# Gram products of a two-layer decoder trunk, taken alternately from the upper and the lower 64 rows of the array

## The chip, the cores and the metric

The kernel runs on one core of one Trainium2 chip, as one launch. The metric is the device time of a launch in microseconds (us), as the median of several runs.

## The reference

Two layers over 512 tokens of width 1024. Each layer projects the normalised input once and gives its columns to three groups of heads that work in parallel: RWKV-7 time mixing (4 heads of 64), retention (4 heads of 64) and latent attention (8 heads). Their outputs are joined, projected and added to the input; a SwiGLU block follows. Cut to the two parts that the change touches:

```python
def rwkv7_step(state, inp):                     # scanned over 512 tokens
    rt, kt, vt, wt, kkt, at = inp
    sa = einsum('bhvk,bhk->bhv', state, -kkt)
    state = state * wt[:, :, None, :] + sa[..., None] * (kkt * at)[:, :, None, :] \
            + vt[..., None] * kt[:, :, None, :]
    return state, einsum('bhvk,bhk->bhv', state, rt)

# retention, chunks of 128 tokens
inner = einsum('bhnqd,bhnkd->bhnqk', qc, kc) * dmask[:, None]
inner = einsum('bhnqk,bhnkd->bhnqd', inner, vc)
cross = einsum('bhnqd,nbhde->bhnqe', qc * q_dec[:, None, :, None], R_prev)
y = inner + cross
```

All is float32.

## The kernel before

Activations lie transposed, features on the partitions and the 512 tokens in the free dimension. The weights stream from HBM block by block (`wnext`): SP issues the load of `wr`, ACT rounds it to `wh` (L375), and DVE forms the rest `wl = wr - wh` (L376). A weight block is used in units of three matmuls, `wh` with both halves of the activation and `wl` with its high half, each 128 rows by 512 tokens (`gemm`, tiles `pd` in PSUM). These big products fill most of the tensor engine's (PE's) time. The block with the retention values is narrower, 288 columns, and its units count 288 instead of 512.

The small work of the three head groups is written as Python generators (`rwkv`, `chain`, `group_norm`, `retnet`, `head`, `attend`). A generator yields a number from the table `T`, how much modelled PE time should pass before it goes on; `Driver` then lets others go, the big gemm last. The order of PE's stream is thus fixed when the kernel is built, from a modelled clock that every `mm` moves on; `keep_in_program_order` holds PE to it. The other engines take their instructions in an order that a scheduler settles at build time. On all engines an instruction that waits holds up those queued behind it.

PSUM has two pools of four one-bank tiles each: `pd` for the big gemm and `pm` for the rest (`psd()`, `psm()`, 128 x 512 float32). A fifth `psm()` waits until the first of the four tiles has been read for the last time.

The recurrence of RWKV-7 is done in chunks of 64 tokens. For each of the 4 heads and 8 chunks a Gram product of 128 x 128 with a contraction of 64 is made (L629): `BK[b]` and `AR[b]` hold two heads each, one on partitions 0 to 63 (`par` 0), one on 64 to 127 (`par` 1). A product therefore uses the upper or the lower 64 rows of the array, and the profile lists two matmul records for it. The loops run over `par`, then `b`, then `i`: four chunks make a block of four products in one `pm` tile. DVE takes the tile out with two masked multiplications of 128 x 256 (L632 into `GL`, L633 into `GR`), and `yield T["rwkv13"]` (0.5) lets one unit of the big gemm go between two blocks. Eight blocks make a layer. After the four of one `par`, SP stores `GL[par]` to the scratch tensor `ms_d` (L635). Behind the last block come the bonus products (`pm<-r,EX`, L640) and the transposes to token-major stacks. SP then loads the 32 x 32 diagonal blocks from `ms_d` into `dg` (L669), and DVE inverts them in 31 steps of two instructions (L679, L680), with a yield after each. Between these steps DVE does the angle tables (L435 to L450), the rotation of the latent attention's key (`kro`, L1010 to L1015; its transposes on PE are the first to need it) and the decayed keys of retention (`kt`, L794).

Retention (`retnet`) scores four chunks of 128 tokens per head (L815): for each pair of heads `b` and each `par` four products of 128 x 128, contraction 64, into one `pm` tile, then a multiplication by the decay mask on DVE (L817), then `yield T["retnet3"]` (0.7). `py` (L824 to L829) uses both heads' masked scores; its products with the values write 64 of the 128 columns, `par` 0 the left and `par` 1 the right half.

Of the kernel before, what the change touches and what calls it, by code (L numbers as in the profile page):

```python
# [16 lines left out]
ALU = mybir.AluOpType  # L17
AX = mybir.AxisListType

P = 128  # L20
# [16 lines left out]
# how much of the tensor engine's work a task leaves between its steps  # L37
T = {'tables1': 19.74, 'norm1': 0, 'p_rwkv': 4, 'p_ret': 1, 'p_head': 4, 'p_tab': 6, 'p_gn': 1, 'p_att': 5, 'p_kr': 6, 'angles1': 0, 'angles2': 3.0, 'angles3': 0.93, 'angles4': 0.65, 'angles5': 2.78, 'angles6': 11.0, 'rwkv1': 2.97, 'rwkv2': 5.34, 'rwkv3': 0, 'rwkv4': 0, 'rwkv5': 4.5, 'rwkv6': 2.0, 'rwkv7': 0, 'rwkv8': 4.0, 'rwkv9': 2.51, 'rwkv10': 1.31, 'rwkv11': 1.12, 'rwkv12': 4.2, 'rwkv13': 0.5, 'rwkv14': 0, 'rwkv15': 0.35, 'rwkv16': 0, 'rwkv17': 0.75, 'rwkv18': 15.07, 'rwkv19': 0, 'rwkv20': 1.0, 'rwkv21': 1.29, 'chain1': 0.9, 'chain2': 0.9, 'chain3': 1.17, 'group_norm1': 3.0, 'group_norm2': 2.5, 'group_norm3': 7.53, 'retnet1': 0.8, 'retnet2': 0, 'retnet3': 0.7, 'retnet4': 3.0, 'retnet5': 2.5, 'retnet6': 0, 'head1': 4.54, 'head2': 0, 'head3': 8.46, 'head4': 0.22, 'attend1': 0, 'key_rope1': 4.96, 'latent_norm1': 1.34, 'latent_norm2': 2.88, 'latent_norm3': 0}
# the engine of each elementwise step that several can do: d DVE, p Pool, a Activation
# [5 lines left out]
def shape_constants():  # L45
    """Constants that depend on shapes and hyper-parameters alone."""
# [10 lines left out]
    j = i % 64  # L57
# [28 lines left out]
# rows of the parameter matrix (one row = 128 consecutive values of a parameter)  # L86
# [15 lines left out]
class Driver:  # L102
    """Orders the PE stream: the first task whose wait (in PE time, or a condition) is over goes on."""
# [25 lines left out]
def lay_out(inp):  # L129
    """The inputs as the kernel reads them: reshapes, transposes and repeated columns only."""  # L130
# [47 lines left out]
def tile_trunk(ctx: ExitStack, tc: tile.TileContext, a: dict, out: bass.AP, dbg=None):  # L178
# [50 lines left out]
    def mm(o, lhsT, rhs, start=True, stop=True, cost=None):  # L229
        """A matmul that keeps its place in the PE stream."""  # L230
# [51 lines left out]
    def split(src, dst):  # L282
        """An exact hi/lo pair of float32r halves."""
# [4 lines left out]
    def halves(src, key, hi_from=None):  # L288
        """The exact hi/lo pair of a tile."""
# [17 lines left out]
    def norm_feed(t, g, acc, tag="acc"):  # L307
        """Square of tile t into acc and the g-scaled tile as an exact hi/lo pair."""
# [14 lines left out]
    def rsqrt(x, y=None):  # L323
        """1 / sqrt(x) of a whole tile, with one Newton step."""
# [7 lines left out]
    def inv_rms(accs, n, tag):  # L332
        """rsqrt(mean + eps) per token, the same in all partitions, from tiles of squares."""
# [7 lines left out]
    def norm(acc, st):  # L341
        yield T["norm1"]
# [9 lines left out]
    # the weights, in order of use, as exact hi/lo pairs two blocks ahead of their products  # L352
# [31 lines left out]
    def gemm(ps, w, x, ks, first=True, last=True, wsl=None):  # L384
        """ps += w^T x in three exact passes; ks = [(index in w, index in x)]."""
# [13 lines left out]
    def first_two(x):  # L399
        """Two products whose last contraction tile comes late."""  # L400
# [847 lines left out]
```

## Time and profile before

| what | value |
|---|---|
| median of 3 runs | 1428.18 us (1426.4 to 1428.36) |
| span of the profiled execution | 1423.1 us |
| mean granted clock of PE | 0.970 of full |
| PE busy | 1366.6 us (96%) |
| DVE busy | 799.1 us (56%) |
| ACT busy | 566.5 us (40%) |
| POOL busy | 267.2 us (19%) |
| masks L632 and L633 | 16 each, 0.41 us each |
| retention masks L817 | 8, 0.68 us each |

The span counts from the first to the last instruction of one execution; the median counts a whole launch, and lies 5.1 us above it. A row of the timeline of an engine gives start, duration, engine, line, operation, output and inputs by the program's names, the form (rows by columns of the array for a matmul, then its operand), and how many instructions of one kind followed each other (x); in brackets stands the idle time before it with the instruction that ended it. A line of a matmul is that of the helper `mm` (L231) or `tr` (L238), so products are told apart by names and forms: `64*128` are the Gram products. Durations of matmuls overlap, since the engine pipelines them; the distance from start to start is what one costs. A row of the view of stretches gives begin and end, length, busy time of PE, of its weight loads (PEld), DVE, ACT and POOL with instruction counts, then the granted clock, the share of DMA and GB/s.

### The profile page before, as it was taken

The numbers are of one execution on the slowest core, as the hardware profiler recorded it, in microseconds if no ns is written. First come the engines' busy times: TensorE is split into PE (matmuls) and PEld (weight loads), VectorE is DVE, ScalarE is ACT, GpSimd is POOL, SyncE is SP. The second block draws the span as 40 slices with busy tenths as digits, with TensorE's granted clock in tenths as the row PEclk, the third lists the DMA queues.
The fourth block names the chain that finished last, engine by engine and source line by source line (L and its number), as shares of the span: only waits on it lengthen the run. The fifth ranks groups of instructions, "written<-read, shape, count | busy, mean of one in ns | idle before, by whom it ended". The sixth has DMA issues, their size and how long they took to land.

```text
span 1423.1 us, 17218 instructions
## 1 busy us (share of the span) xinstructions
PE 1366.6 (96%) x6622; PEld 1074.5 (76%) x6622; DVE 799.1 (56%) x1167; ACT 566.5 (40%) x943; POOL 267.2 (19%) x233
## 2 busy tenths in 40 slices
PE   7989899899999999999999989999999999999996
PEld 5768666568788888888887776765788888888884
DVE  6665855775644345444556767657475434543443
ACT  7633353663432223222457134448263322322233
POOL 2142024222211011001213502332031200100111
PEclk9869999999999999999999899999999999999998
DMA  6324231202332232322342332312123333333321
GB/s 224 90 81 112 76 92 53 91 36 77 104 102 95 98 98 95 103 89 93 118 138 77 107 87 56 100 43 75 59 89 104 89 104 93 100 98 95 100 77 60
DMA packets 61738, 130.85 MB, mean 92 GB/s; under 512 B 24948, under 2 KB 27668, under 8 KB 61656
## 3 DMA queue, kind: packets, MB, share of 16 engines
q1 hardware_dynamic: 60280, 128.14, 29.1%
q8 instruction: 52, 0.85, 0.3%
q10 hardware_dynamic: 1232, 1.09, 0.2%
q0 software_dynamic: 144, 0.52, 0.1%
q14 instruction: 30, 0.25, 0.1%
HBM read 117.40 MB, written 9.18 MB: 89 GB/s over the span
## 4 chain that ended last, share of the span: by engine, by line
PE 83%; DVE 8%; ACT 4%; issue 3%; POOL 1%; DMA 0%; SPq 0%; DVEq 0%; ACTq 0%; POOLq 0%
PE pd L231 70%; PE pm L231 12%; PE pm L238 1%; DVE r L680 1%; ACT wh L375 1%; DVE u L320 1%; DVE r L679 1%; DMA wr<-in_wts_dram 0%; DVE wl L376 0%; ACT u L860 0%; DVE nmx L858 0%; DVE u L286 0%; DVE r L295 0%; DVE r L328 0%; DVE r L329 0%
## 5 line engine op out<-in xcount | busy, mean ns | idle before, releaser
L231 PE MATMUL pd<-u,wh 128*128 128x512 f32 x3048 | 963.6, 397 | 9.9 <-ACT wh L375 6.3
L231 PEld LDWEIGHTS pd<-u,wh 128*128 128x128 f32 x3048 | 571.2, 190 | 139.8 <-issue 8.3
L231 PE MATMUL pd<-u,wl 128*128 128x512 f32 x1524 | 598.8, 393 | 0.0
L375 ACT CAST wh<-wr 128x1024 fp32r<-128x1024 f32 (+3 forms) x206 | 208.6, 1015 | 547.0 <-PE pd L231 349.2
L231 PEld LDWEIGHTS pd<-u,wl 128*128 128x128 f32 x1524 | 289.3, 190 | 61.3 <-DVE wl L376 0.2
L376 DVE TENSOR_TENSOR wl<-wr,wh 128x1024 fp32r<-128x1024 f32 (+3 forms) x198 | 277.6, 1404 | 82.9 <-ACT wh L375 82.1
L1184 POOL TENSOR_TENSOR r<-r,r 128x512 f32<-128x512 f32 x44 | 62.3, 1416 | 584.3 <-ACT wh L375 337.5
L1183 DVE TENSOR_TENSOR r<-pd,rB 128x512 f32<-128x512 f32 x44 | 30.4, 691 | 133.7 <-PE pd L231 133.7
L1190 DVE TENSOR_TENSOR u<-u,pd 128x512 f32<-128x512 f32 x48 | 33.0, 687 | 125.8 <-PE pd L231 125.8
L231 PE MATMUL pm<-u,u 32*32 32x32 f32 (+7 forms) x856 | 97.3, 279 | 5.8 <-DVE u L607 4.3
L231 PEld LDWEIGHTS pm<-u,u 32*32 32x32 f32 (+4 forms) x856 | 70.1, 155 | 41.5 <-issue 25.2
L315 POOL TENSOR_TENSOR acc<-acc,r 128x512 f32<-128x512 f32 x37 | 56.8, 1534 | 221.5 <-ACT r L314 221.0
L1181 DVE TENSOR_TENSOR r<-pd,rB 128x512 f32<-128x512 f32 x44 | 30.4, 691 | 68.4 <-PE pd L231 68.3
L285 ACT CAST u<-r 128x512 fp32r<-128x512 f32 x52 | 32.2, 622 | 63.0 <-POOL r L1184 62.8
L231 PE MATMUL pd<-u,u 96*128 96x512 f32 (+3 forms) x128 | 47.7, 471 | 1.9 <-ACT u L860 1.3
L286 DVE TENSOR_TENSOR u<-r,u 128x512 fp32r<-128x512 f32 x52 | 36.4, 701 | 16.5 <-ACT u L285 16.3
L376 POOL TENSOR_TENSOR wl<-wr,wh 128x1024 fp32r<-128x1024 f32 (+1 forms) x8 | 19.7, 2460 | 116.8 <-ACT wh L375 98.9
L238 PE MATMUL pm<-ident,u 128*128 128x128 f32 x188 | 35.2, 295 | 2.7 <-ACT u L875 1.8
L858 DVE TENSOR_REDUCE nmx<-pd 128x1 f32<-128x512 f32 (+1 forms) x64 | 30.0, 481 | 12.1 <-PE pd L231 11.9
L320 DVE SCALAR_TENSOR_TENSOR u<-u,PC,u 128x512 fp32r<-128x512 f32 x24 | 34.5, 1450 | 3.0 <-ACT u L319 3.0
L238 PEld LDWEIGHTS pm<-ident,u 128*128 128x128 f32 x188 | 25.1, 153 | 9.5 <-ACT u L875 2.2
L745 POOL TENSOR_SCALAR sd<-Sb,dsc 64x64 f32<-64x64 f32 x48 | 23.9, 498 | 42.2 <-DVE Sb L746 33.6
(241 smaller groups left out, 1170.6 us busy)
## 6 DMA issues: line engine op xcount, KB each, us to landing
wr<-in_wts_dram SPq DMA_DIRECT2D x174, 512.0 KB, 3.5
wr<-in_wts_dram SPq DMA_DIRECT2D x22, 384.0 KB, 3.1
u<-in_xT_dram SPq DMA_DIRECT2D x7, 512.0 KB, 7.1
tb<-tab_d SPq DMA_DIRECT2D x8, 256.0 KB, 3.4
r<-r SPq DMA_DIRECT2D x32, 64.0 KB, 2.0
h_d<-u SPq DMA_DIRECT2D x4, 512.0 KB, 2.6
u<-h_d SPq DMA_DIRECT2D x4, 512.0 KB, 4.9
wr<-in_wts_dram SPq DMA_DIRECT2D x4, 432.0 KB, 3.1
```

The lines of the kernel that those rows point to most:

```text
L231: tc.keep_in_program_order(nc.tensor.matmul(o, lhsT, rhs, start=start, stop=stop, skip_group_check=True))
L238: tc.keep_in_program_order(nc.tensor.transpose(o, x, idn))
L285: act.copy(hi, src)
L286: E("e273").tensor_tensor(lo, src, hi.bitcast(F32), ALU.subtract)
L315: E("e302").tensor_tensor(acc, acc, q, ALU.add)
L320: dve.scalar_tensor_tensor(lo, t, g, hi.bitcast(F32), ALU.mult, ALU.subtract)
L375: act.copy(hi[:, z], t[:, z])
L376: (pool if on in POOL_LO else dve).tensor_tensor(lo[:, z], t[:, z], hi[:, z].bitcast(F32), ALU.subtract)
L1181: dve.tensor_tensor(t, gu[0], rB, ALU.mult)
L1183: dve.tensor_tensor(u, gu[1], rB, ALU.mult)
L1184: E("e1171").tensor_tensor(t, t, u, ALU.mult)
L1190: dve.tensor_tensor(hk(m), hk(m), ps, ALU.add)
```

## The change

In the recurrence the loop over `par` moves inside. A step takes two `pm` tiles, one per `par`, and makes eight products, one into the first tile from rows 0 to 63, one into the second from rows 64 to 127, in turns. Four masks follow on DVE, then one yield; four steps make a layer, with a unit of the big gemm behind each. Both stores to `ms_d` come behind the last step. Retention's scores do the same per pair of heads: two tiles, eight products in turns, then two masks with a yield behind each. Nothing of the values changes. `T` becomes a list with one table per layer, both as the one before; line numbers move by one to three.

```diff
-        for par in range(2):
-            rows = slice(par * 64, par * 64 + 64)
-            for b in range(2):
-                for i in range(2):
-                    ps = psm()
-                    for j in range(4):
-                        n = 4 * i + j
-                        mm(ps[:, j * P : (j + 1) * P], BK[b][rows, n, :], AR[b][rows, n, :])
-                    h0 = b * 8 + 4 * i
-                    v3 = ps.rearrange("p (j w t) -> p j w t", j=4, w=2)
-                    dve.tensor_tensor(GL[par][:, h0 : h0 + 4, :], v3[:, :, 0, :], gmv[:, 0:1, :].broadcast_to([P, 4, 64]), ALU.mult)
-                    dve.tensor_tensor(GR[par][:, h0 : h0 + 4, :], v3[:, :, 1, :], gmv[:, 1:2, :].broadcast_to([P, 4, 64]), ALU.mult)
-                    yield T["rwkv13"]
-            sp.dma_start(ms_d[:, par * 16 : par * 16 + 16, :], GL[par][0:64])
+        GH = (slice(0, 64), slice(64, 128))
+        for b in range(2):
+            for i in range(2):
+                pg = [psm(), psm()]
+                for j in range(4):
+                    n = 4 * i + j
+                    for ps, rows in zip(pg, GH):
+                        mm(ps[:, j * P : (j + 1) * P], BK[b][rows, n, :], AR[b][rows, n, :])
+                h0 = b * 8 + 4 * i
+                v3 = [ps.rearrange("p (j w t) -> p j w t", j=4, w=2) for ps in pg]
+                for par in range(2):
+                    dve.tensor_tensor(GL[par][:, h0 : h0 + 4, :], v3[par][:, :, 0, :], gmv[:, 0:1, :].broadcast_to([P, 4, 64]), ALU.mult)
+                    dve.tensor_tensor(GR[par][:, h0 : h0 + 4, :], v3[par][:, :, 1, :], gmv[:, 1:2, :].broadcast_to([P, 4, 64]), ALU.mult)
+                yield T[l]["rwkv13"]
+        for par in range(2):
+            sp.dma_start(ms_d[:, par * 16 : par * 16 + 16, :], GL[par][0:64])
...
         for b in range(2):
-            Sm = []
+            Sm, pg = [], [psm(), psm()]
+            for n in range(4):
+                tk = slice(n * P, (n + 1) * P)
+                for par in range(2):
+                    rows = slice(par * 64, par * 64 + 64)
+                    mm(pg[par][:, tk], ks[rows, b, tk], qs[rows, b, tk])
             for par in range(2):
-                hh = 2 * b + par
-                rows = slice(par * 64, par * 64 + 64)
-                ps = psm()
-                for n in range(4):
-                    tk = slice(n * P, (n + 1) * P)
-                    mm(ps[:, tk], ks[rows, b, tk], qs[rows, b, tk])
+                hh, ps = 2 * b + par, pg[par]
                 t = r2()
```

PE's order around the first blocks of layer 0, before. `pm` tiles with a number are Gram blocks (`u_632` is `AR[0]`, `u_633` is `BK[0]`), `pd` rows are the gemm's units:

```order
L231 MATMUL pd_702<-u_143,wl_506 128x512
L231 MATMUL pm_735<-u_632,u_633 128x128 x4
L231 MATMUL pd_702<-u_146,wh_505 128x512 x2
L231 MATMUL pd_702<-u_146,wl_506 128x512
L231 MATMUL pm_746<-u_632,u_633 128x128 x4
L231 MATMUL pd_764<-u_112,wh_600 128x512 x2
L231 MATMUL pd_764<-u_112,wl_601 128x512
L231 MATMUL pm_774<-u_673,u_674 128x128 x4
```

And now, from the first step's last products to the next step's:

```order
L232 MATMUL pm_735<-u_632,u_633 128x128
L232 MATMUL pm_736<-u_632,u_633 128x128
L232 MATMUL pd_702<-u_146,wh_505 128x512 x2
L232 MATMUL pd_702<-u_146,wl_506 128x512
L232 MATMUL pm_753<-u_632,u_633 128x128
L232 MATMUL pm_754<-u_632,u_633 128x128
```

Where four products into one tile stood between two units, eight now stand, each other one into the second tile; the step behind the next unit takes the third and the fourth tile of the pool.

DVE's order in layer 0, before, from the weight split ahead of the Gram masks to the second block's masks (`u_731` and `u_732` are `GL`, `u_733` and `u_734` are `GR`):

```order
L376 TENSOR_TENSOR wl_705<-wr_703,wh_704 128x1024
L295 TENSOR_TENSOR r_142_684<-r_139_680,r_141_683 128x512
L614 SCALAR_TENSOR_TENSOR r_140_681<-u_498,PC,u_294 128x512
L376 TENSOR_TENSOR wl_767<-wr_765,wh_766 128x864
L295 TENSOR_TENSOR r_144_689<-r_140_681,r_143_688 128x512
L978 TENSOR_TENSOR r_145_692<-pd_598,rB_259 128x512
L632 TENSOR_TENSOR u_731<-pm_735,C 128x256
L633 TENSOR_TENSOR u_733<-pm_735,C 128x256
L632 TENSOR_TENSOR u_731<-pm_746,C 128x256
L633 TENSOR_TENSOR u_733<-pm_746,C 128x256
```

And now:

```order
L377 TENSOR_TENSOR wl_705<-wr_703,wh_704 128x1024
L377 TENSOR_TENSOR wl_781<-wr_779,wh_780 128x864
L296 TENSOR_TENSOR r_142_684<-r_139_680,r_141_683 128x512
L615 SCALAR_TENSOR_TENSOR r_140_681<-u_498,PC,u_294 128x512
L296 TENSOR_TENSOR r_144_689<-r_140_681,r_143_688 128x512
L981 TENSOR_TENSOR r_145_692<-pd_598,rB_259 128x512
L634 TENSOR_TENSOR u_731<-pm_735,C 128x256
L635 TENSOR_TENSOR u_733<-pm_735,C 128x256
L634 TENSOR_TENSOR u_732<-pm_736,C 128x256
L635 TENSOR_TENSOR u_734<-pm_736,C 128x256
L634 TENSOR_TENSOR u_731<-pm_753,C 128x256
```

The second weight split has moved up by two rows; both tiles of a step are masked one after the other, and the masks of the second step follow at once.

SP's order behind the Gram products of layer 0, before (`r` rows are swaps for the rotation of retention's queries and keys, `u_919` is `dg`, `wr` is a weight):

```order
L635 DMA ms_d<-u_731 64x1024
L980 DMA r_158_754<-r_157_753 32x512 x4
L635 DMA ms_d<-u_732 64x1024
L980 DMA r_177_866<-r_176_865 32x512 x4
L372 DMA wr_1074<-in_wts_dram 128x1024
L669 DMA u_919<-ms_d 32x32x32 x4
```

And now (`u_890` is `dg`):

```order
L983 DMA r_160_768<-r_159_767 32x512 x4
L638 DMA ms_d<-u_731 64x1024
L638 DMA ms_d<-u_732 64x1024
L672 DMA u_890<-ms_d 32x32x32 x4
L373 DMA wr_1078<-in_wts_dram 128x1024
```

Both stores stand together, and the loads of the diagonal blocks follow at once, ahead of the weight that they stood behind.

More of the change, by code (lines that the diff above doesn't have):

```diff
@@ L339, in inv_rms, with norm @@
         return rsqrt(x, sm((P, S), tag=tag, bufs=1))
-    def norm(acc, st):
-        yield T["norm1"]
+    def norm(l, acc, st):
+        yield T[l]["norm1"]
         st["rB"] = inv_rms(acc if isinstance(acc, list) else [acc], D, "rB")
@@ L417, in tables @@
     def tables():
-        yield T["tables1"]
+        yield T[0]["tables1"]
         posi = r2((P, S), I32)
@@ L464, in tables @@
         ready["ret"] = True
-        yield T["angles5"]
+        yield T[0]["angles5"]
         yield from angles(None, True)
         ready["kr"] = True
-        yield T["angles6"]
+        yield T[0]["angles6"]
         co, si = yield from angles(c("invm"))
@@ L532, in rwkv @@
         k_ = rkv["k"]
-        yield T["rwkv5"]
+        yield T[l]["rwkv5"]
         kk = ur([P, 2, S])
@@ L749, in chain @@
             E("c736").copy(AR[b][:, n, 64:128], pY)
-            yield T["chain3"]
-        drv.spawn(T["p_gn"], group_norm(l, st, b))
+            yield T[l]["chain3"]
+        drv.spawn(T[l]["p_gn"], group_norm(l, st, b))
     def group_norm(l, st, b):
@@ L818, in retnet @@
                 Sm.append(t)
-                yield T["retnet3"]
-            yield T["retnet4"]
+                yield T[l]["retnet3"]
+            yield T[l]["retnet4"]
             py = psm()
@@ L863, in head @@
             (pool if ib == 2 else dve).tensor_scalar(pp[ib], pp[ib], rs, None, ALU.mult)
-            yield T["head2"]
-        yield T["head3"]
+            yield T[l]["head2"]
+        yield T[l]["head3"]
         ta, tb = ur([P, 1024]), r2()
@@ L879, in head @@
         if hh ^ 1 in st["PT"]:
-            drv.spawn(T["p_att"], attend(l, st, b))
+            drv.spawn(T[l]["p_att"], attend(l, st, b))
     def attend(l, st, b):
-        yield T["attend1"]
+        yield T[l]["attend1"]
         po = psm()
@@ L931, in dense @@
             mix = st["mix"]
-            drv.spawn(T["p_rwkv"], rwkv(l, st))
-            drv.spawn(T["p_ret"], retnet(l, st))
+            drv.spawn(T[l]["p_rwkv"], rwkv(l, st))
+            drv.spawn(T[l]["p_ret"], retnet(l, st))
             for hh in range(8):
-                drv.spawn(T["p_head"], head(l, st, hh // 2, hh % 2))
+                drv.spawn(T[l]["p_head"], head(l, st, hh // 2, hh % 2))
             pss = yield from first_two(xg)
-            drv.spawn(0, norm(acc, st))
+            drv.spawn(0, norm(l, acc, st))
             ps = psd()
```

83 lines of the change are left out of this document (42 added, 41 removed).

## The prediction

> **What bounds the kernel now.** First the page: the busy shares, and the chain of work that ended last.
>
> ```profile
> PE 1366.6 (96%) x6622; PEld 1074.5 (76%) x6622; DVE 799.1 (56%) x1167; ACT 566.5 (40%) x943; POOL 267.2 (19%) x233
> PE 83%; DVE 8%; ACT 4%; issue 3%; POOL 1%; DMA 0%; SPq 0%; DVEq 0%; ACTq 0%; POOLq 0%
> ```
>
> PE works 96% of the span and carries 83% of the chain: time taken off PE comes off the end, unless a wait takes its place. Next one group by line and form, and two of PE's waits:
>
> ```profile
> L231 PE MATMUL pm<-u,u 64*128 64x128 f32 x192 | 36.9, 349 | 5.8 <-DVE u L607 4.3 <-DVE u L633 1.5
> PE pm L238 <- DVE kro L1015: 6.6, 1, 6.6
> PE pm L231 <- DVE kt L794: 5.5, 5, 3.0
> ```
>
> The first row is the change's object: 192 matmul records for 96 Gram products (two each), on 64 of the 128 rows. The third figure of that row is idle time before the group: PE waited 4.3 us for the products' inputs (L607) and 1.5 us for a PSUM buffer (which L633 had to empty). The timeline of PE gives the stretch in layer 0:
>
> ```profile
> 82.10 1.34 PE L231 MATMUL pm<-u,u 64*128 64x128 f32 x8 [4.30 <-DVE u L607]
> 83.37 1.22 PE L231 MATMUL pd<-u,wh 128*128 128x512 f32 x2
> 84.95 2.07 PE L231 MATMUL pm<-u,u 64*128 64x128 f32 x8
> 86.95 1.22 PE L231 MATMUL pd<-u,wh 128*128 128x512 f32 x2
> ...
> 109.87 1.91 PE L231 MATMUL pm<-r,EX 128*128 128x512 f32 x4
> ```
>
> Eight blocks of four products (x8 records), and behind each a unit of the big gemm (three matmuls). From start to start a block takes 86.95 - 84.95 = 2.00 us and a unit 84.95 - 83.37 = 1.58; the bonus products (pm<-r,EX) begin at 109.87. Why this is slow, the view of stretches says; the first figure behind POOL's is the granted clock:
>
> ```profile
> 82.87:113.59 30.72, 30.72 (x95) 22.64 (x94) 15.54 (x30) 2.75 (x5) 5.92 (x6) 0.50 0.24 62
> 113.59:144.00 30.41, 26.85 (x168) 24.18 (x166) 18.02 (x26) 12.16 (x21) 10.66 (x10) 1.00 0.50 122
> 803.08:816.73 13.65, 13.65 (x52) 11.93 (x52) 7.01 (x14) 0.47 (x2) 5.41 (x7) 0.50 0.46 123
> ```
>
> PE is busy without a gap from 82.87 to 113.59, but at half clock. The clock stays there while half-array blocks come and is full again 113.59 - 109.87 = 3.7 us after the whole-array bonus products begin. The two slow stretches are 9 and 4 times 3.41 us long, so the clock changes on a grid of 3.4 us.
>
> **What a pair of products costs after the change.** No row of before has alternating row halves. The nearest has two column halves, in retention's output (its weight loads are the last row):
>
> ```profile
> 171.11 0.44 PE L231 MATMUL pm<-r,u 128*64 128x128 f32 x4
> 171.48 0.49 PE L231 MATMUL pm<-r,Rs 128*128 128x128 f32 x2
> 171.90 0.44 PE L231 MATMUL pm<-r,u 128*64 128x128 f32 x4
> 171.11 0.20 PEld L231 LDWEIGHTS pm<-r,u 128*64 128x64 f32 x4 [0.35 <-DVE r L680]
> ```
>
> Two products on two column halves (x4) take 171.48 - 171.11 = 0.37 us; one on the whole array (x2) takes 171.90 - 171.48 = 0.42. A pair costs no more than a single product, and its four weight loads lie within 0.20 us. I therefore let eight products on two row halves take the time that four on one half take now. The other end is no overlap at all: every product at its present price. The Trainium skill (TensorEngine Tiling (Array Packing), Key Properties) says that different tiles can load weights and multiply in parallel, and that changing the tiling mode, not just the tile, drains TensorE. By it alternating halves is free and only the start of a block costs, the end that I take; for column halves the trace agrees (0.37 us a pair), for row halves no row shows it.
>
> **Layer 0.** Four steps of eight products, a unit behind each. Steps 1 and 2 run as blocks 1 and 2 do (82.10, 84.95), and the unit behind step 2 ends at 86.95 + 1.58 = 88.53. Step 3 needs two PSUM tiles while steps 1 and 2 hold all four of the pool: it waits until DVE has emptied step 1's. DVE's timeline:
>
> ```profile
> 89.99 0.41 DVE L632 TENSOR_TENSOR u<-pm,C 128x256 f32<-128x256 f32 x1
> ...
> 90.98 0.41 DVE L633 TENSOR_TENSOR u<-pm,C 128x256 f32<-128x256 f32 x1
> ```
>
> DVE reaches the first mask at 89.99; the change puts one weight split a few rows earlier ahead of it, which DVE did before 89.99 anyhow. The fourth mask ends at 90.98 + 0.41 = 91.4, so PE waits 91.4 - 88.5 = 2.9 us where it didn't wait before. Step 3, unit, step 4, unit at half clock are 2.0 + 1.6 + 2.0 + 1.6 = 7.2: the bonus begins near 98.6, with half a microsecond for what lies between engines at 99.2. That is 10.7 us ahead, but only four units have been done where there were eight. What a unit costs at full clock is in these rows (139.60 - 138.92 = 0.68):
>
> ```profile
> 138.92 0.62 PE L231 MATMUL pd<-u,wh 128*128 128x512 f32 x2
> 139.60 0.62 PE L231 MATMUL pd<-u,wh 128*128 128x512 f32 x2
> ```
>
> The four that are owed take 2.7 us once the clock is back, and when that is decides. The grid from 82.87 gives 96.5, 99.9 or 103.35. At 99.9, 0.7 us of the bonus stretch has run at half clock, where before 3.7 had: the other 3.0 take 1.5 at full clock, so the state of 113.59 is reached at 99.9 + 1.5 + 2.7 = 104.1, a gain of **9.5 us**. At 103.35 the same sum gives 7.8, at 96.5 11.1; and if the denser steps bring the clock back at once, step 3 onwards takes half, and 13.6 comes out. I take 99.9: packed steps use all rows, like the bonus products that ended the slow stretch, but the wait at 88.5 leaves PE idle.
>
> The Trainium skill (TensorEngine Tiling (Array Packing), PSUM Bottleneck) speaks against the change: tiling speeds up TensorE but not the emptying of PSUM. By it the steps would go at DVE's pace. From the rows above four masks take 1.4 us, a step and its unit 3.6 at half clock and about 2.0 at full, so in this trace it bites only in the wait of step 3.
>
> **What hangs on the Gram stores.** SP now issues both stores to scratch behind the last step, and the loads of the diagonal blocks right after them, ahead of the next weight. The second store waits for the last mask in both kernels, and that comes about 10 us earlier, so the loads behind it do too. DVE begins the triangular inverse one weight split earlier:
>
> ```profile
> 132.07 1.23 DVE L376 TENSOR_TENSOR wl<-wr,wh 128x1024 fp32r<-128x1024 f32 x1 [3.50 <-ACT wh L375]
> 133.21 0.20 DVE L679 TENSOR_TENSOR r<-u,r 128x31 f32<-128x31 f32 x1
> ...
> 146.75 0.21 DVE L1015 TENSOR_TENSOR kro<-kro,kro 128x64 f32<-128x64 f32 x1
> ```
>
> PE's 6.6 us wait for kro is the end of 13.7 us of DVE work, inverse and angles interleaved, from 133.21 to 146.96. The split at 132.07 now falls into it instead of ahead of it. Both the splits and PE move up with the weights, so the wait stays: 0, between 3 us better (a start one split sooner, held by the slower interleave) and 2 us worse.
>
> **Retention.** Blocks of four products, two per pair of heads:
>
> ```profile
> 162.34 1.16 PE L231 MATMUL pm<-u,u 64*128 64x128 f32 x8
> 163.43 0.73 PE L231 MATMUL pd<-u,wh 128*128 128x512 f32 x2
> ...
> 165.02 1.16 PE L231 MATMUL pm<-u,u 64*128 64x128 f32 x8
> ```
>
> A block is 1.09 us at full clock. Two become one, four times over both layers: 4 x 1.09 = 4.4 us at most. A single product took 0.42 above, so a further one costs (1.09 - 0.42) / 3 = 0.22 and the start of a block 0.2: without overlap only four starts go, 0.8. Taken: **4.0**. The second mask now comes earlier for its reader, two units sooner.
>
> **Layer 1.** The same eight blocks, at first at full clock (the last row is DVE's first mask):
>
> ```profile
> 791.45 1.16 PE L231 MATMUL pm<-u,u 64*128 64x128 f32 x8
> 792.53 0.73 PE L231 MATMUL pd<-u,wh 128*128 128x512 f32 x2
> 793.43 1.16 PE L231 MATMUL pm<-u,u 64*128 64x128 f32 x8
> ...
> 800.93 1.13 PE L231 MATMUL pm<-u,u 64*128 64x128 f32 x8 [1.50 <-DVE u L633]
> 813.81 1.91 PE L231 MATMUL pm<-r,EX 128*128 128x512 f32 x4
> 800.04 0.41 DVE L632 TENSOR_TENSOR u<-pm,C 128x256 f32<-128x256 f32 x1
> ```
>
> DVE is late here: its first mask starts at 800.04, so four end at 801.4. Steps 1 and 2 with their units take 2 x 1.98 and end at 795.4: the 1.5 us wait becomes one of 6, and the clock falls, as it did after the 4.3 us wait of layer 0. The same 7.2 us at half clock bring the bonus to 808.6, against 813.81. Owed are one unit and three pairs of units 288 columns wide instead of 512, 0.68 x (1 + 6 x 288 / 512) = 3.0 us. On the grid from 803.08 the clock is back at 809.9: 1.3 us of the bonus stretch at half clock, against 816.73 - 813.81 = 2.9 before, and the state of 816.73 is reached at 809.9 + 0.8 + 3.0 = 813.7. Gain **3.0 us**; back only at 813.3, 1.3; never fallen, 6.8.
>
> **Sum.** 9.5 + 4.0 + 3.0 = 16.5 us. The profiled execution spans 1423.1; the median, 1428.18, lies 5.1 above it, which I take as constant: 1428.2 - 16.5 = **1411.7 us**.
>
> **Rivals.** *Waits eat it* (0.14). DVE works through its backlog in the order written and PE arrives sooner, so it waits longer for masks, and later for kro and kt: layers 0 and 1 give half (6.2 us) and retention 1: 1421.0. For it: the 6 us wait above, and 6.6 + 5.5 us of waits for kro and kt that are DVE's already. Against: DVE is busy 15.54 us of the 30.72 in the layer 0 stretch.
>
> *The halves don't overlap* (0.09). Then only starts go: with 0.4 for a start at half clock and 0.2 at full, and 0.2 that a unit begins slower behind a block (792.53 to 793.43 is 0.90, against 0.68), 4 x 0.6 + 4 x 0.5 + 4 x 0.3 = 5.6: 1422.6. Against it stand the 0.37 us of the column halves.
>
> *Each change of half drains the array* (0.05), slower: every product costs a start. Layer 0 32 x 0.4, layer 1 16 x 0.2 + 16 x 0.4, retention 32 x 0.2 are 28.8 us, less the 5.6 saved: 1451.4. With nothing overlapped it decides from 5.6 / 96 = 0.06 us a change. The drain rule named above would give this time if the other row half counted as another mode; the column halves speak against it.
>
> *The clock stays up* (0.10): packed steps count as full use; 13.6 + 6.8 + 4.4 = 24.8: 1403.4.
>
> **How the numbers follow.** The forecast has 0.62, with a range of its own of 1405 to 1419: from 7.8 + 0.8 + 1.3 to 11.1 + 4.4 + 6.8, and a microsecond for kro. The whole range takes in the clock case, the waits and the missing overlap, and leaves out the drain and the far ends: 1402 to 1424. Under 0.2% (2.9 us) a measurement can't tell a difference from none. Faster: the forecast, the clock, most of the missing overlap and of the waits, 0.85. Within: waits that take nearly all, 0.07. Slower: the drain, and waits for DVE's inverse beyond that, 0.08.
>
> **What would show it.** Gram groups of x16 in about 1.1 us at full clock and 2.0 at half; layer 0's bonus near 99; waits of PE for the masks of about 3 us before step 3 in layer 0 and 6 us in layer 1; kro's wait as before. The forecast is wrong if x16 takes 2 us or more at full clock (no overlap), if kro's or kt's wait grows by more than 3 us, or if the clock of 82.87 to 98 is well over 0.5.

## The result and the profile after

The changed kernel takes 1435.03 us (1434.44 to 1435.61), the kernel before 1428.27 beside it: a ratio of 1.0056, 95% interval [1.0041, 1.0072]. It is slower by some 7 to 8 us, where 16.5 us faster had been forecast. The profiled execution spans 1432.6 us against 1423.1, granted clock 0.965 against 0.970. In every run of these kernels a launch takes 1.8 us more than its own execution spans, so the profiled execution of the kernel before was a short one, by this estimate a launch of 1424.9 us, and comparisons of single traces with it show a kernel some 2 to 5 us worse than the medians do.

The page, after, gives PE fewer busy microseconds in a longer span. In the chain that ended last PE has less (83% before, 79% now) and DVE more (8% before, 11% now):

```profile
PE 1358.4 (95%) x6622; PEld 1065.6 (74%) x6622; DVE 794.4 (55%) x1167; ACT 571.9 (40%) x947; POOL 263.3 (18%) x233
PE 79%; DVE 11%; ACT 5%; issue 2%; DMA 1%; POOL 1%; SPq 0%; DVEq 0%; ACTq 0%; POOLq 0%
```

The Gram products themselves did what was forecast. Their group, by line and form, after:

```profile
L232 PE MATMUL pm<-u,u 64*128 64x128 f32 x192 | 20.3, 356 | 12.6 <-DVE u L635 8.3 <-DVE u L608 4.3
```

36.9 us busy have become 20.3; the idle time before the group has grown from 5.8 to 12.6. The timeline of PE in layer 0, after:

```profile
81.17 2.17 PE L232 MATMUL pm<-u,u 64*128 64x128 f32 x16 [4.30 <-DVE u L608]
83.27 1.22 PE L232 MATMUL pd<-u,wh 128*128 128x512 f32 x2
84.85 2.08 PE L232 MATMUL pm<-u,u 64*128 64x128 f32 x16
...
90.85 0.46 PE L232 MATMUL pm<-u,u 64*128 64x128 f32 x2 [2.62 <-DVE u L635]
...
98.29 1.09 PE L232 MATMUL pm<-r,EX 128*128 128x512 f32 x4
129.44 0.39 PE L232 MATMUL pd<-u,wl 128*128 128x512 f32 x1
139.43 0.80 PE L239 MATMUL pm<-ident,kro 128*32 128x128 f32 x3 [9.61 <-DVE kro L1018]
```

Sixteen records in 2.08 us at half clock, as eight took before; PE waits 2.6 us for the masks before step 3 (forecast: 2.9), and the bonus starts at 98.3 (forecast: 99.2; the changed kernel reaches the first Gram product 0.9 us earlier than the kernel before, so the stretch is as long as forecast). Up to the unit at 129.44 the forecast holds. Then the wait for kro is 9.6 us, not 6.6. Further on, around retention's second output, on PE and on DVE:

```profile
174.69 0.43 PE L232 MATMUL pm<-r,u 128*64 128x128 f32 x2
177.78 0.43 PE L232 MATMUL pm<-r,u 128*64 128x128 f32 x2 [2.66 <-DVE r L820]
...
180.28 0.70 PE L232 MATMUL pm<-r,u 128*64 128x128 f32 x4
180.91 3.62 PE L232 MATMUL pm<-u,u 32*32 32x32 f32 x64
```

```profile
175.91 1.22 DVE L377 TENSOR_TENSOR wl<-wr,wh 128x1024 fp32r<-128x1024 f32 x1 [2.15 <-ACT wh L376]
177.05 0.68 DVE L820 TENSOR_TENSOR r<-pm,C 128x512 f32<-128x512 f32 x1
```

The same place on PE in the kernel before:

```profile
187.20 0.43 PE L231 MATMUL pm<-r,u 128*64 128x128 f32 x2 [1.12 <-DVE r L817]
...
189.92 0.72 PE L231 MATMUL pd<-u,wh 128*128 128x512 f32 x2
...
193.36 2.21 PE L231 MATMUL pm<-u,u 32*32 32x32 f32 x64
```

PE now waits 2.66 us for the second mask instead of 1.12. On DVE that mask is queued behind a weight split that itself waits for ACT. Behind the output the 32 x 32 products of the inverse now follow at once; before, the gemm units from 189.92 on stood between. The granted clock in stretches of the changed kernel:

```profile
80.94:98.01 17.07, 14.01 (x75) 10.86 (x76) 14.41 (x28) 2.47 (x4) 6.38 (x8) 0.60 0.28 79
176.52:179.93 3.41, 2.15 (x15) 1.39 (x16) 3.34 (x6) 2.56 (x5) 0.00 (x0) 1.00 0.02 7
179.93:193.58 13.65, 13.65 (x129) 10.70 (x129) 5.23 (x8) 5.39 (x9) 1.27 (x1) 0.50 0.12 30
866.01:883.08 17.07, 15.38 (x53) 10.34 (x54) 9.36 (x16) 6.92 (x11) 2.93 (x2) 0.70 0.38 79
896.73:903.56 6.83, 6.83 (x53) 4.30 (x52) 2.89 (x5) 1.67 (x3) 1.26 (x1) 0.50 0.39 89
```

The Gram stretch has the clock back early, but from 179.93 on PE works 13.65 us without a gap at half clock. Layer 1 has less of it: 10.2 of the 17.07 us from 866.01 (at a mean of 0.70), and 6.83 us from 896.73. The kernel before was at full clock from 151.1 to 280.8 and from 816.7 to 980.6, which takes in the matching places. The Trainium skill (TensorE: Matmul & The Clock Gate, Part 1) lets the clock fall after an idle window of about 3.4 us. Here it fell after a window in which PE was busy for 2.15 of 3.41 us, and stayed down with no idle time at all while products of 32 rows and units alternated. The 32-row products alone don't bring it down: in r11, told below, the same 64 follow the output at full clock, behind a wait of 1.15 us for the mask.

```profile
188.56 2.21 PE L231 MATMUL pm<-u,u 32*32 32x32 f32 x64
```

Where the time went shows best when the same matmul is found in both traces: the n-th `wl` matmul of the big gemm, counted from the start, narrow units too. The table gives its start less that in the kernel before, in us, from one execution each; the last columns belong to runs told below.

| n | what lies between this row and the one above | changed | r2 | r5 | r7 | r8 | r11 | r12 |
|---|---|---|---|---|---|---|---|---|
| 68 | all ahead of layer 0's Grams | -0.9 | 0.6 | -0.4 | 1.5 | -0.9 | -0.7 | -0.6 |
| 128 | Grams, bonus, transposes | -10.6 | 0.6 | -12.8 | -10.3 | -14.9 | -0.9 | -10.4 |
| 132 | kro | -8.1 | 0.7 | -14.4 | -11.8 | -16.2 | -1.4 | -8.0 |
| 156 | retention's scores | -11.0 | -1.9 | -16.8 | -13.5 | -18.6 | -1.4 | -10.8 |
| 240 | outputs, chain, most of attention | -0.1 | -0.8 | -15.5 | -10.9 | -14.5 | 3.0 | -6.7 |
| 884 | the rest, up to layer 1's Grams | 1.5 | 0.8 | -12.2 | -9.3 | -12.9 | 1.5 | -5.1 |
| 936 | Grams, kro | -3.4 | 0.9 | -17.5 | -14.2 | -18.5 | 2.7 | -10.0 |
| 956 | retention's scores | -4.1 | -0.4 | -18.8 | -14.1 | -17.9 | 3.5 | -10.7 |
| 1040 | outputs, chain, attention | 9.6 | 4.0 | -14.4 | -9.6 | -17.9 | 13.9 | -5.4 |

The changed kernel gains 9.7 us in the first stretch and 4.9 in layer 1's; it loses 10.9 between 156 and 240, 1.6 more by 884, and 13.7 between 956 and 1040, nearly all of it in work that the change doesn't touch. The two stretches that lose most, from n = 156 to 240 and from 956 to 1040, in the kernel before, the changed one and r11:

```profile
181.90:334.81 152.91, 146.77 (x931) 100.99 (x930) 95.56 (x201) 80.33 (x192) 40.87 (x48) 0.99 0.23 71
866.24:1022.61 156.37, 149.55 (x952) 104.63 (x950) 101.36 (x213) 82.66 (x197) 42.30 (x45) 0.98 0.23 66
```

```profile
170.95:334.67 163.72, 154.94 (x932) 106.11 (x930) 92.04 (x202) 82.97 (x195) 40.12 (x48) 0.94 0.19 61
862.19:1032.17 169.98, 157.36 (x952) 107.39 (x950) 100.57 (x212) 85.47 (x199) 39.95 (x45) 0.94 0.21 60
```

```profile
180.48:337.80 157.32, 149.45 (x931) 101.63 (x931) 92.23 (x201) 82.77 (x194) 39.25 (x48) 0.98 0.22 69
869.70:1036.50 166.80, 153.82 (x951) 106.02 (x951) 101.64 (x213) 87.02 (x199) 41.33 (x45) 0.97 0.21 62
```

The length less PE's busy time is PE's idle time. In the changed kernel both stretches together are 24.4 us longer; 8.4 of these are idle time. The clock is at half for 41.0 us of them instead of 10.2; since work takes twice as long at half clock (2.08 us for sixteen Gram records, 1.09 at full), this comes to some 15.4 us, an estimate. So in this trace nearly two thirds of the loss are half clock.

### The profile page after: what moved, and what is told of

Same layout as the page of the kernel before. It is cut to its first block, busy times and chain, and to the rows that moved or that the text cites. A ratio compares the mean times of both kernels' runs of the same rounds, so it can differ in the third digit from the quotient of the medians.

```text
span 1432.6 us, 17225 instructions
## 1 busy us (share of the span) xinstructions
PE 1358.4 (95%) x6622; PEld 1065.6 (74%) x6622; DVE 794.4 (55%) x1167; ACT 571.9 (40%) x947; POOL 263.3 (18%) x233
## 3 DMA queue, kind: packets, MB, share of 16 engines
q10 hardware_dynamic: 1232, 1.09, 0.2%
## 4 chain that ended last, share of the span: by engine, by line
PE 79%; DVE 11%; ACT 5%; issue 2%; DMA 1%; POOL 1%; SPq 0%; DVEq 0%; ACTq 0%; POOLq 0%
PE pd L232 68%; PE pm L232 10%; PE pm L239 1%; DVE wl L377 1%; DVE r L683 1%; DVE r L682 1%; ACT wh L376 1%; DVE nmx L861 1%; DVE u L321 1%; ACT u L863 1%; DMA wr<-in_wts_dram 1%; ACT L327 0%; DVE r L329 0%; DVE u L287 0%; DVE u L607 0%
## 5 line engine op out<-in xcount | busy, mean ns | idle before, releaser
L232 PE MATMUL pm<-u,u 32*32 32x32 f32 (+7 forms) x856 | 87.4, 292 | 15.3 <-DVE u L635 8.3
L232 PEld LDWEIGHTS pm<-u,u 32*32 32x32 f32 (+4 forms) x856 | 60.5, 165 | 50.6 <-issue 31.0
L861 DVE TENSOR_REDUCE nmx<-pd 128x1 f32<-128x512 f32 (+1 forms) x64 | 30.1, 480 | 10.9 <-PE pd L232 10.4
L748 POOL TENSOR_SCALAR sd<-Sb,dsc 64x64 f32<-64x64 f32 x48 | 23.4, 487 | 48.3 <-DVE Sb L749 40.2
L239 PEld LDWEIGHTS pm<-ident,u 128*128 128x128 f32 x188 | 24.0, 146 | 10.3 <-ACT u L878 2.6
```

The costliest lines, as they stand in the source:

```text
L232: tc.keep_in_program_order(nc.tensor.matmul(o, lhsT, rhs, start=start, stop=stop, skip_group_check=True))
L239: tc.keep_in_program_order(nc.tensor.transpose(o, x, idn))
L861: dve.tensor_reduce(nmx, ps[:, 0:w], AX.X, ALU.max, negate=True)
```

## The experiments

Three theories stood at the start. A: the order. Four steps with one yield each leave four gemm units between the Gram products where eight had been; the recurrence's later products are placed by the same modelled clock, so they now stand some four units earlier against the gemm, where the work that they need isn't ready, or where they no longer fill a wait. B: retention's packed scores bring PE to its masks too early. C: DVE sets the pace, and what PE saves anywhere it waits for later. The place of a product is told as the number of gemm units ahead of it in PE's order:

| | bonus, layer 0 and 1 | 32 x 32 products, layer 0 and 1 |
|---|---|---|
| before | 79, 896 | 166, 986 |
| changed | 75, 889 | 162, 981 |
| r4 (yield 0.7) | 79, 893 | 166, 982 |
| r5 to r10 (yield 1.2 or list) | 79, 896 | 166, 986 |
| r11 (before, shifted) | 79, 896 | 162, 982 |
| r12 (changed, shift undone) | 75, 889 | 166, 986 |

### r1: the recurrence alone

Retention's scores are those of the kernel before:

```diff
-            Sm, pg = [], [psm(), psm()]
...
+            Sm = []
             for par in range(2):
...
+                ps = psm()
```

> Only the recurrence is packed; retention's scores are as before. Theory A (order): the four gemm units that no longer stand between the Gram steps shift the recurrence's later products, so that the 32 x 32 products follow retention's output directly, and PE waits there at half clock. Then 1433 to 1441 us, no better than the changed kernel, with the 13.7 us stretch at half clock behind the second retention output of layer 0 still there. Theory B (retention): PE reaches retention's masks too early because of the packed scores; then 1412 to 1419. Theory C (DVE's pace): what PE saves it waits for later in any version; then 1425 to 1431.

Measured: 1435.02 us, ratio 1.0038 [1.0018, 1.0058]. B falls as the sole cause: without retention's packing the loss is about the same. A's half clock behind the second output did not come back in this run's trace, though, which has the full clock from 169 to 190. The loss stood elsewhere, in layer 1 and in the attention: PE waited 4.7 us for the exponentials of the softmax, 1.3 before. The profiled execution took 1430.5 us, 4.5 less than the median, so nothing shows whether the longer ones lack the half clock too.

### r2: retention alone

The recurrence's loop over `par` with its eight blocks is back, retention stays packed:

```diff
-                pg = [psm(), psm()]
...
+        for par in range(2):
+            rows = slice(par * 64, par * 64 + 64)
+            for b in range(2):
```

> Only retention's scores are packed; the recurrence has its eight blocks and eight units as before. Theory A: 1423 to 1428, retention keeps the 2 to 4 us that its blocks save, no stretch at half clock behind the outputs. Theory B: slower, 1432 to 1440, with longer waits for retention's masks and the half clock behind them. Theory C: 1427 to 1430.

Measured: 1428.21 us, 0.9991 [0.998, 1.0001], no difference. C had said 1427 to 1430 and holds for this run; A had said 1423 to 1428 and just misses, B is off. In the table r2 gains 2.6 us at layer 0's scores and 1.3 at layer 1's, and gives 4.4 back behind 956, where PE waits 3.60 us for the second mask instead of 1.66 and the clock is at half for 6.83 us from 878.9. Packed retention alone shows no gain at the end.

### r3: two tiles, but one half after the other

```diff
-                for j in range(4):
-                    n = 4 * i + j
-                    for ps, rows in zip(pg, GH):
+                for ps, rows in zip(pg, GH):
+                    for j in range(4):
+                        n = 4 * i + j
```

and the same in retention's scores.

> The changed kernel with its two tiles, its four steps and its order, but the four products of the upper rows all come before the four of the lower rows, so that only one pair per step can overlap. Theory A: the Gram savings go and the order's cost stays, 1440 to 1450, with the layer 0 bonus near 106. Theory B: PE reaches the masks about as late as before, 1424 to 1430. Theory C: 1427 to 1431. If it takes as long as the changed kernel, the overlap of the halves is worth nothing at the end.

Measured: 1435.28 us, 1.0046 [1.003, 1.0063], the time of the changed kernel. It lies outside all three ranges; the last sentence of the expectation applies. In this order the overlap of the halves is worth nothing at the end.

### r4: two units behind each step

In both tables of `T` one entry changes (the rest of the line is left out here and in r5, r11 and r12):

```diff
-'rwkv13': 0.5
+'rwkv13': 0.7
```

> The changed kernel with the yield behind a Gram step raised from 0.5 to 0.7, so that two gemm units instead of one follow each step: eight units in the stretch as before, and all later products of the recurrence stand against the gemm as they did before. Theory A: faster, 1411 to 1419, no half clock behind retention's outputs, PE's wait before step 3 shorter by about 1.5 us in both layers. Theory B: 1428 to 1436, the half clock stays. Theory C: 1425 to 1431, with the saved time found again as waits of PE for DVE.

Measured: 1420.46 us, 0.994 [0.9923, 0.9956]: faster than before, by one number of the table of yields. It is 1.5 us above A's range. The table of places suggests why, and r5 tests it: in layer 1, where units are narrower, 0.7 still leaves the recurrence three to four units early. Two signs that A named did not come: the waits before step 3 are 2.6 and 5.3 us, against 2.6 and 5.5 in the changed kernel, and from retention's second output on the clock is at half again, for 6.83 us, with no 32-row products there.

```profile
171.30:178.13 6.83, 6.26 (x24) 4.00 (x25) 2.85 (x5) 1.66 (x4) 0.00 (x0) 0.50 0.28 62
```

### r5: the whole order kept

```diff
-'rwkv13': 0.5
+'rwkv13': 1.2
```

Every later product of PE now stands behind the same unit as in the kernel before, in both layers.

> The changed kernel with the yield behind a Gram step at 1.2 instead of 0.5: all later products on PE stand behind exactly the gemm unit behind which they stood before, in both layers (at 0.7 the second layer's recurrence still ran four units early). Theory A (order): what the run with 0.7 lost between the 32 x 32 products and the attention of layer 1, some 9 us, is not lost: 1409 to 1415 us. Theory C (DVE's pace): no better than with 0.7, 1418 to 1423.

Measured: 1411.61 us, 0.9893 [0.9873, 0.9913]. A holds and C falls: the same packing, the same DVE work, 23 us less than the changed kernel.

### r6: the whole order kept, recurrence alone

r5 with retention's scores as before (the edit of r1).

> The same with retention's scores as before, so that only the recurrence is packed. If packed retention costs PE its wait for the second mask of layer 1 and the half clock behind it (4.3 us in two runs, against 1.3 us gained at the products), this is 0 to 4 us faster than the run with both: 1407 to 1413. If retention's packing pays as I predicted, it is 4 us slower: 1413 to 1419.

Measured: 1412.83 us, 0.9897 [0.9876, 0.9917]. It lies at the upper end of the first range, 1.2 us from r5 with overlapping intervals: packed retention again makes no difference that can be told.

### r7: the whole order kept, one half after the other

r3 with the yield of 1.2.

> Both parts in the changed kernel's two tiles and four steps, order kept by the yield of 1.2, but the four products of one half before the four of the other, so that the halves hardly overlap. It prices the overlap by itself. Theory A: the overlap is worth something at the end once the order is kept, 6 to 12 us, so 1418 to 1425 here. If the overlap is worth nothing at the end, as the two runs in the changed order suggest (1435.0 and 1435.3), then the same as the run with both packed, 1409 to 1415.

Measured: 1413.24 us, 0.9907 [0.989, 0.9924]. The expectation of A for the overlap fell: it is worth 1.6 us by the medians, and the intervals overlap. Yet the step alone is much shorter when the halves alternate. Layer 0's second step in r7, and then in r5, both at full clock:

```profile
88.38 1.71 PE L232 MATMUL pm<-u,u 64*128 64x128 f32 x16
90.02 0.73 PE L232 MATMUL pd<-u,wh 128*128 128x512 f32 x2
```

```profile
86.05 1.16 PE L232 MATMUL pm<-u,u 64*128 64x128 f32 x16
87.14 0.73 PE L232 MATMUL pd<-u,wh 128*128 128x512 f32 x2
```

1.64 us against 1.09: 0.55 for each of twelve steps, 6.6 us for the kernel at full clock. Where they go, PE's waits for the masks of the Gram stretch show, r7 first, then r5:

```profile
PE pm L232 <- DVE u L635: 4.5, 2, 2.8
```

```profile
PE pm L232 <- DVE u L635: 6.9, 4, 3.9
```

The order with overlap, r5, waits 2.4 us more in the Gram stretches of both layers. The rest of the 6.6 is not assigned to single waits. The Trainium skill (TensorEngine Tiling (Array Packing), PSUM Bottleneck) says that tiling speeds up TensorE and not the emptying of PSUM. r5 and r7 agree in part: of 6.6 us saved on PE 2.4 go into longer waits for the masks that empty PSUM, and 1.6 arrive at the end.

What brought r7 its 14 us, then, is for the most part not the overlap of alternating halves but the grouping: eight half-array products and then two whole-array units, where four and one had alternated. The granted clock over the Gram stretch of layer 0 in r7:

```profile
84.41:101.40 16.99, 15.28 (x85) 12.06 (x83) 13.90 (x28) 2.06 (x3) 4.62 (x5) 0.80 0.31 84
```

0.80, where the kernel before had 0.50 for 30.7 us. In r7 6.8 us of the stretch are at half clock; the 23.9 us fewer would save half of that, 12.0, an estimate, and the table has 11.8 (from 1.5 to -10.3), though PE waits 1.7 us more there, so that some 1.5 us have another source. Single traces could differ by where the 3.41 us grid falls, but they agree. The three with four products and one unit (before, r2, r11) have 30.72 us at half clock:

```profile
83.62:114.34 30.72, 30.72 (x95) 22.51 (x94) 15.42 (x30) 2.99 (x5) 5.78 (x6) 0.50 0.24 62
81.01:111.73 30.72, 30.37 (x93) 22.59 (x94) 16.06 (x30) 2.59 (x4) 7.03 (x6) 0.50 0.24 63
```

The eleven with eight products have 3.4 to 20.5 us. The 20.5 are r3's, halves in turn with one unit behind a step; with one unit and alternating halves (changed, r1, r12) it is 13.7. So with one unit the overlap shortens the half clock too, and with two units r7 has as little as r5.

### r8: retention packed in layer 0 only, order kept

r5 with the loop of the kernel before for `l > 0` in retention's scores:

```diff
+            Sm, pg = [], [psm(), psm()] if l == 0 else []
+            for n in range(4 if l == 0 else 0):
...
+                if l > 0:
+                    rows = slice(par * 64, par * 64 + 64)
+                    pg.append(psm())
```

> Order kept by the yield of 1.2, recurrence packed in both layers, retention packed in layer 0 only. If layer 1's second mask is what spoils packed retention, this is the fastest, 1 to 3 us below the run with the recurrence alone packed: 1405 to 1411. If layer 0's retention has the same fault, it is as that run or slower, 1409 to 1415.

Measured: 1408.03 us, 0.9871 [0.9851, 0.9892], in the range of the first case. The 4.4 us that r5 loses behind 956 are not lost (-17.9 stays -17.9 in the table). Only part of that can be put down to the unpacked scores. PE's wait for the second mask of layer 1 is 3.58 us in r5 and 1.66 in r8, as it is in r6; but in r6 the clock falls behind that shorter wait too:

```profile
861.06 0.69 PE L232 MATMUL pm<-r,u 128*64 128x128 f32 x2 [3.58 <-DVE r L820]
```

```profile
865.52 0.43 PE L232 MATMUL pm<-r,u 128*64 128x128 f32 x2 [1.66 <-DVE r L820]
866.30:873.13 6.83, 6.83 (x25) 4.73 (x25) 2.94 (x5) 1.09 (x2) 0.00 (x0) 0.50 0.13 45
```

r9, with the scores of r8, has the same 6.83 us at half clock from 859.3; r8 and r10 have none there. So about 1.9 us are the mask's, and that r8's trace kept the clock is not shown to come from the scores. The intervals of r8, r5 and r6 overlap, so their order is by medians.

### r9 and r10: the units put where PE waits

r9 is r8, r10 is r6, with a list of yields for the four steps:

```diff
-                yield T[l]["rwkv13"]
+                yield (0, 3.8, 0, 1.2)[2 * b + i]
```

> As the run with retention packed in layer 0 only and the order kept, but the gemm units of the Gram stretch stand where PE waits for the masks: steps 1 and 2 directly behind each other, then six units (seven in layer 1), steps 3 and 4, then the rest. If units can fill the waits before step 3 (1.3 us in layer 0, 3.9 us in layer 1), 3 to 6 us faster than that run: 1402 to 1405 us. If DVE's pace sets the end of the stretch, the wait moves to the bonus products and the time stays at 1407 to 1410.

> The same placing of the units with retention's scores as before in both layers. Waits filled: 3 to 6 us faster than the recurrence alone with the order kept (1412.8), so 1407 to 1410. Waits only moved: 1411 to 1414.

Measured: r9 1408.18 us, 0.9868 [0.9852, 0.9885]; r10 1411.64, 0.9893 [0.9877, 0.9908]. No better than r8 and, within the noise, than r6: the waits moved. PE's row for kro in r9 and r8:

```profile
132.42 1.04 PE L239 MATMUL pm<-ident,kro 128*32 128x128 f32 x4 [7.19 <-DVE kro L1024]
```

```profile
130.45 1.03 PE L239 MATMUL pm<-ident,kro 128*32 128x128 f32 x4 [4.86 <-DVE kro L1024]
```

PE reaches kro at much the same time in both (125.2 and 125.6, the start less the wait), but in r9 DVE has it ready 2.0 us later, and PE waits 7.2 us instead of 4.9. To this extent C was right: at kro, DVE's work sets the time.

### r11: the kernel before, with the shift alone

Nothing is packed; one number, the yield ahead of the inverse's 32 x 32 products:

```diff
-'rwkv18': 15.07
+'rwkv18': 12.3
```

> The kernel before, with nothing packed, but the yield ahead of the 32 x 32 products of the inverse lowered from 15.07 to 12.3: the recurrence's products from there on stand four gemm units earlier, in layer 0 exactly where the changed kernel has them. Theory A (order, from the inverse on): slower than before by 6 to 14 us, 1434 to 1442, with half clock behind retention's second output or more waits in the attention of both layers. If the loss of the changed kernel comes from DVE's order ahead of the key rotation instead, or from packing itself, no change: 1425 to 1431.

Measured: 1439.89 us, 1.0091 [1.0076, 1.0106], 12 us slower, in A's range. A shift of this size thus costs 12 us without any edit of the changed kernel. Of the two places that A named it is the second: the clock stays full behind retention's output, and the loss stands in the attention. PE's waits there, before and in r11 (L860 is the exponential of the softmax, on ACT), and the longest of r11:

```profile
PE pd L231 <- ACT u L860: 1.3, 4, 0.5
```

```profile
PE pd L231 <- ACT u L860: 8.4, 7, 3.3
```

```profile
1004.41 1.13 PE L231 MATMUL pd<-u,u 96*128 96x512 f32 x2 [3.27 <-ACT u L860]
```

8.4 us against 1.3 before. By the rows of the two stretches shown with the result, r11 loses 14.8 us there: 7.9 are idle time, 17.1 us at half clock instead of 10.2 make some 3.4, and 3.5 are not assigned. The changed kernel loses by the same shift more through the clock. That the chain of the recurrence, ending four units earlier, no longer fills the attention's waits fits these rows, but no run shows it by itself.

### r12: the changed kernel, with the shift undone behind the inverse

```diff
-'rwkv18': 15.07
+'rwkv18': 18.7
...
-'rwkv18': 15.07
+'rwkv18': 19.5
```

> The changed kernel, with the yield ahead of the 32 x 32 products raised (18.7 in layer 0, 19.5 in layer 1) so that from there on every product of the recurrence stands behind the same gemm unit as before; the stretch ahead of it stays as changed, the key rotation on DVE behind twelve inverse steps too. Theory A: most of the loss is gone, 1416 to 1422, and what is left to the run with the whole order kept (1411.6) is the longer wait for the key rotation, 4.7 us, and the Gram stretch. If DVE's order ahead of the key rotation is the cause, 1429 to 1436.

Measured: 1420.31 us, 0.9948 [0.9935, 0.9961]. With the 32 x 32 products and all behind them back at their units, 14.7 of the 23.4 us between the changed kernel and r5 are recovered. What remains is seen in the table: kro (9.6 us of waiting here, 4.9 in r5) and the Gram stretches. r12 first, then r5:

```profile
PE pm L239 <- DVE kro L1018: 9.6, 1, 9.6
```

```profile
PE pm L239 <- DVE kro L1018: 4.9, 1, 4.9
```

## Why the prediction was wrong

**What held.** A pair on two row halves costs what one product costs (16 records in 2.08 us at half clock, 1.09 at full, as eight records did before). Layer 0's Gram stretch was forecast to give 9.5 us and gave 9.7 (from -0.9 to -10.6). The waits before step 3 were forecast at 2.9 and 6 us; they were 2.6 and 5.5. Layer 1's stretch gave 4.9, forecast 3.0. The rivals of no overlap, of a drain at each change of half, and of a clock that stays up did not come. The clock in layer 0 was not quite as taken: it was full from 87.8 to 91.2, mostly while PE waited, so that the mean was 0.60, and it was back at 98.0. Counted from the first Gram product this is 98.9 in the forecast, where 99.9 had been taken; by its own sum that is worth 0.3 us. The 5.1 us between span and median, taken as constant, are 1.8 us between span and launch and a short execution; the forecast subtracts from the median and doesn't depend on them.

**The step that failed** is in the part on layer 0: "The four that are owed take 2.7 us once the clock is back". It took the gemm units that no longer stand between the steps as work that is merely done later, at its plain price. They are also what places the rest of the recurrence. The bonus moved from unit 79 to 75 and from 896 to 889, the 32 x 32 products from 166 to 162 and 986 to 981, while kro's transposes (129, 931) and retention's scores (142, 944) stayed at theirs. No term of the sum had a price for that, though the order of PE could have been read for it. r11 shows the part of this shift from the inverse on to cost 12 us by itself, r12 that undoing that part in the changed kernel brings back 14.7, and r5 that with the whole order kept the same packing gives 1411.6, which is the time that was forecast, reached by other sums than the forecast's, so that agreement is luck.

**kro**: taken at 0, between 3 us better and 2 worse; the wait grew from 6.6 to 9.6 us, and unit 132 was 2.5 us worse than 128. DVE finished kro with 22 inverse instructions ahead of it instead of 15. The prediction saw that the inverse starts one split earlier, but took this to move both ends alike.

**Retention**: the scores gave 2.9 us in layer 0 and 0.7 in layer 1 up to unit 956, forecast 4.0 for both. But PE then waited for the second mask, 2.66 us instead of 1.12 in layer 0. The prediction said that this mask comes earlier for its reader; it overlooked that the mask is queued on DVE behind a weight split (175.91) that waits for ACT, and does not move with PE. r2 and r6 show the sum: nothing that can be told.

**The clock** was treated only inside the Gram stretch. The half clock from 179.93, 13.65 us long, lies far behind it, after the wait for the mask and the 32-row products that the shift put there. r1's trace is 5.7 us longer than that before without this stretch, and r12 is free of all but 3.4 us of it, so it is one form that the loss took in the changed kernel, not its only cause. r1 is known by one execution, a short one. The forecast had no term for half clock outside the Gram stretches, and by the estimate above this is some 15 us of what the changed kernel's trace loses.

**The rival "waits eat it"** had the right direction but not the right mechanism and size: it let waits return half of the gain, at most all of it. That a shift of the order can cost more than the change saves was not among the rivals; the 0.08 for the slower side stood for the drain and for waits for the inverse.

**The explanation of the gain** was off as well. The forecast put it to the overlap. r7 shows that, once the order is kept, nearly all of it is there with the halves one after the other, from the grouping that lets the clock come back in layer 0; r5 and r7 differ by 1.6 us.

What stays open: why the shift costs where it does. The sum is shown by r11 and r12, and the traces divide it between idle time and half clock; which of the shifted products each wait hangs on, and what part DVE's changed order has in it, no run separates.

## What to carry to other kernels

When a change removes points at which other work is let in, count what later work is placed by those points, and compare the order behind the change with the one before: a shift of four gemm units cost 12 us in a kernel with nothing else changed, and in the packed kernel the order decided between 7 us slower and 16 us faster. A time table tuned to one order is part of the kernel; retune the numbers that the change invalidates before judging the change (0.5 to 1.2 took it from 1435 to 1411.6 us). And what a packed step saves on its engine reaches the end only as far as those that empty and read it keep up: 6.6 us on PE were 1.6 at the end.

## What the runs showed of the hardware

Products that alternate between the two row halves of the array overlap: 16 records take 1.09 us, as eight on one half did before, against 1.64 when the halves come one after the other. The clock came back to full inside the Gram stretch when eight half-array products were followed by two whole-array units (0.80 over the stretch of r7), although the halves came one after the other there; with four and one it stayed at half for 30.72 us in three traces, with PE busy 30.37 to 30.72 us of it. The clock fell behind a wait of 2.66 us (the changed kernel, 179.93) and behind one of 1.66 us (r6, 866.30), and behind the same 1.66 us it did not in r8 and r10.
